# A hybrid decoder layer whose input x also comes transposed from the host, with the first weight tiles used for both token halves at once

## The chip, the cores and the metric

The kernel runs on one core of one Trainium2 chip. The time is device time of one execution in microseconds (us), from a few timed runs; beside it stands one execution recorded by the hardware profiler.

PE is the matrix engine (TensorE), DVE the vector engine, ACT the scalar engine, POOL the GpSimd engine, and SP the queue that issues most loads. Each engine works its instructions off in a fixed order and waits, where it must, at the head of that order. TensorE has two clock levels, 1.2 and 2.4 GHz.

## The reference

The input x has 256 tokens of 2048 features in float32. Three residual stages follow one another, and this study touches only the start of the first:

```python
def swiglu(x, w_gate, w_up, w_down):
    return (jax.nn.silu(x @ w_gate) * (x @ w_up)) @ w_down

def reference(x, ...):
    alpha = (2.0 * DEPTH) ** 0.25
    x = layer_norm(alpha * x + 0.5 * swiglu(x, ffn1_w_gate, ffn1_w_up, ffn1_w_down), ln1_g, ln1_b)
    p = x @ w_in
    mix = concat(diff_attn_group(p[..., :3072], ...), rwkv7_group(p[..., 3072:], ...)) @ w_out
    x = layer_norm(alpha * x + mix, ln2_g, ln2_b)
    return layer_norm(alpha * x + 0.5 * swiglu(x, ffn2_w_gate, ffn2_w_up, ffn2_w_down), ln3_g, ln3_b)
```

The gate and up weights are 2048 x 5632, the down weights 5632 x 2048.

## The kernel before

Nearly all time goes into matrix products of the 256 tokens with streamed weights. The tokens are worked in two halves of 128 (tt = 0 and 1), the weights in column blocks of 512. A block runs over 16 row chunks of 128 (k), two of them per step, so a step loads one weight tile `raw` of 128 x 2 x 512 (512 KB) through SP. To get nearly full float32 precision, each operand is split into a high part of the reduced type fp32r and the rest: ACT copies `raw` to `wh` (line 121), DVE subtracts to get `wl` (line 122), and each product takes three matmuls (lines 103 to 105): high x high, high x rest of the weight, rest of x x high. So one step of one token half is 2 x 3 = 6 matmuls of 512 columns, accumulated in one PSUM bank `acc`; there are 3 such banks.

`raw` has 3 buffers, `wh` and `wl` have 7 each: a load can be issued once the `wl` of three tiles earlier is made, and a `wh` can be written once PE is through with the tile seven earlier. The second token half runs behind the first by LAG = 4 steps (`pend`).

For the matmul x must lie with its features on the partitions. `load_x` loads a piece of 128 tokens x 512 features (256 KB, 8 pieces in all) by hooks at certain steps, `transpose_split` lets PE transpose it in four 128 x 128 pieces into PSUM (line 70), and `split` makes `xh` (line 76, on ACT, and on DVE for the first two pieces) and `xl` (line 77, DVE) from PSUM.

When a gate block ends, ACT makes `sg`, its silu (line 206), out of `acc`; when an up block ends, DVE makes `h` from `sg` and `acc` (line 211), PE transposes it (line 214), and it is split again. The steps run gate block, up block, gate block and so on.

The order of the instructions on each engine isn't the order of the code: a scheduler sets it when the kernel is built, from its own estimate of durations. At the start POOL also loads small constants, and `lp`, `ls`, `le` and `neglam` (lines 293 to 315) are made from them.

Of the kernel before, what the change touches and what calls it, by code (L numbers as in the profile page):

```python
# [10 lines left out]
F32 = mybir.dt.float32  # L11
F32R = mybir.dt.float32r
AF = mybir.ActivationFunctionType
ALU = mybir.AluOpType
AX = mybir.AxisListType

P = 128
D = 2048
S = 256
# [11 lines left out]
LAG = 4  # L31
NW = 7
# [5 lines left out]
def build(tc, A, out):  # L38
# [11 lines left out]
    def nm(s):  # L50
        uid[0] += 1
        return f"{s}_{uid[0]}"
# [14 lines left out]
    def transpose_split(src, tt, q, store, on_dve=False):  # L67
        tr = tr_bank[-1]()
        for j in range(4):
            T.transpose(tr[:, j, :], src[:, j * P:(j + 1) * P], ident)  # L70
        split(tr, store, tt, q, on_dve)
# [12 lines left out]
    class Stream:  # L84
# [24 lines left out]
        def block(self, src, c0, w, ks, lhs, done, budget=0.0):  # L109
            blk = dict(ks=ks, w=w, lhs=lhs, done=done)  # L110
            for ki in range(0, len(ks), 2):
                for f in self.hooks.get(self.step, ()):
                    f()
                self.step += 1
                n = 2
                r0 = ks[ki][0]
                raw = wp.tile([P, n, NB], F32, tag="raw", name=nm("raw"), bufs=NRAW)
                nc.sync.dma_start(out=raw[:, :, :w], in_=src[r0 * P:(r0 + n) * P, c0:c0 + w].rearrange("(k p) n -> p k n", p=P))
                wh = wp.tile([P, n, NB], F32R, tag="wh", name=nm("wh"), bufs=NW)
                wl = wp.tile([P, n, NB], F32R, tag="wl", name=nm("wl"), bufs=NW)  # L120
                SC.copy(out=wh[:, :, :w], in_=raw[:, :, :w])  # L121
                V.tensor_tensor(out=wl[:, :, :w], in0=raw[:, :, :w], in1=wh[:, :, :w].bitcast(F32), op=ALU.subtract)  # L122
                st = (blk, ki, n, wh, wl)
                self.mm(st, 0)
                self.pend.append(st)
                if len(self.pend) > LAG:
                    self.mm(self.pend.pop(0), 1)
                self.run_bg(budget)

# [170 lines left out]
    def mix(mp, pq, C):  # L300
# [16 lines left out]
        # --- evacuation of a column block into channel-major layout  # L317
# [21 lines left out]
        # --- LoRA inputs  # L339
# [108 lines left out]
        def rwkv_group(g, st):  # L448
# [21 lines left out]
            # decay products: exp of sums of log decays, inside a chunk  # L470
# [12 lines left out]
            # keys  # L483
# [30 lines left out]
            # receptance  # L514
# [15 lines left out]
            # pairwise products inside a chunk  # L530
# [9 lines left out]
            # inverses of the 32x32 diagonal blocks, one block per partition  # L540
# [67 lines left out]
            # chunk recurrence  # L608
# [49 lines left out]
            # group norm, bonus, gate  # L658
# [46 lines left out]
        # --- attention  # L705
# [21 lines left out]
        def attn_heads(g, st, heads):  # L727
# [3 lines left out]
            for h in heads:  # L731
# [38 lines left out]
                # mean square in two ranges, so that it overflows to a zero scale as float32 does, with no infinity formed  # L770
# [91 lines left out]
    with tc.tile_pool(name="fp1", bufs=1) as fp, tc.tile_pool(name="pt1", bufs=4, space=bass.MemoryType.PSUM) as pt:  # L862
        tr_bank.append(ffn_bank(pt))
        xc = [fp.tile([P, D], F32, tag=f"y{tt}", name=nm("xc")) for tt in range(2)]

        def load_x(tt, q):
            c = slice(q * NB, (q + 1) * NB)
            nc.sync.dma_start(out=xc[tt][:, c], in_=A["x"][0, tt * P:(tt + 1) * P, c])
            transpose_split(xc[tt][:, c], tt, q, xT, tt == 0 and q < 2)

        for q in range(4):
            stream.hooks[2 * q] = [lambda q=q: load_x(0, q)]
        for q in range(4):
            stream.hooks.setdefault(2 * q + LAG, []).append(lambda q=q: load_x(1, q))
# [15 lines left out]
_INS = ["x", "ffn1_w_gate", "ffn1_w_up", "ffn1_w_down", "ln1_g", "ln1_b", "w_in", "lambda_q1", "lambda_k1",  # L890
# [34 lines left out]
```

## Time and profile before

| | |
|---|---|
| median of 3 runs | 2044.84 us (2044.75 to 2050.93) |
| the profiled execution, first to last instruction (span) | 2040.2 us |
| PE busy | 2005.6 us |
| DVE busy | 1149.2 us |
| ACT busy | 884.8 us |
| moved by DMA | 373.35 MB, mean 183 GB/s |

The profiled execution is known by its span alone; what lies around it (launch and end) is not timed apart. The median of the runs stands 4.6 us above the span. Busy time is the time in which an engine ran at least one instruction. Matmuls overlap in the array: a matmul of 512 columns is shown 0.39 us long, and the next one starts 0.226 us after it, so the distance of two starts is what counts.

### The profile page before, as it was taken

The page shows a single profiled execution, that of the slowest core. Times are in us where ns is not written, and L with a number is a line of the kernel's source. Part 1 is how long each engine was busy: PE and PEld are TensorE (multiplying, and loading weights), DVE is VectorE, ACT ScalarE, POOL GpSimd, SP SyncE. Part 2 cuts the span into 40 slices and gives each one's busy share as a digit, 9 for nine tenths or more (in the row PEclk, how much of TensorE's full clock was granted, in tenths as well). Part 3 has the DMA queues.
Part 4 walks back from the last instruction along what each step waited for, and adds up shares of the span by engine and source line. Part 5 has one row for each costly group of instructions (what it writes and reads, how often), then busy time and mean ns, then how long its engine had stood idle before and what let it go on. Part 6 is the DMA issues. An engine that isn't in the chain of part 4 may idle for free.

```text
span 2040.2 us, 24921 instructions
## 1 busy us (share of the span) xinstructions
PE 2005.6 (98%) x9671; PEld 1631.2 (80%) x9671; DVE 1149.2 (56%) x1419; ACT 884.8 (43%) x1097; POOL 33.5 (2%) x67
## 2 busy tenths in 40 slices
PE   8999999999999999999999989999999999999997
PEld 6888888888888878887778767788888888888886
DVE  5555444445545576776577856755545444454555
ACT  4444443344444337546474533444444334444432
POOL 2000000000000000000000000000000000000000
PEclk9999999999999999999999969999999999999999
DMA  7666656667666556565436715666666666766653
GB/s 248 199 188 192 186 190 201 204 191 228 193 186 190 188 176 194 172 171 154 116 95 175 217 37 174 194 204 187 186 187 192 202 203 196 227 187 186 192 189 124
DMA packets 201992, 373.35 MB, mean 183 GB/s; under 512 B 22810, under 2 KB 24928, under 8 KB 201104
## 3 DMA queue, kind: packets, MB, share of 16 engines
q1 hardware_dynamic: 182912, 350.53, 56.7%
q10 hardware_dynamic: 17440, 14.29, 2.5%
q0 software_dynamic: 1520, 6.93, 0.9%
q8 instruction: 76, 1.25, 0.3%
q14 instruction: 44, 0.36, 0.0%
HBM read 364.10 MB, written 7.60 MB: 182 GB/s over the span
## 4 chain that ended last, share of the span: by engine, by line
PE 90%; DVE 5%; DMA 2%; ACT 1%; issue 1%; SPq 0%; DVEq 0%; ACTq 0%
PE acc L105 28%; PE acc L103 28%; PE acc L104 28%; DVE wl L122 1%; PE tr L214 1%; DMA raw<-in_w_out_dram 1%; PE sm L653 1%; PE sm L650 1%; PE sm L536 1%; DVE y L177 0%; PE tr L325 0%; PE at L741 0%; DMA xc<-in_x_dram 0%; DVE y L178 0%; DVE Y L560 0%
## 5 line engine op out<-in xcount | busy, mean ns | idle before, releaser
L122 DVE TENSOR_TENSOR wl<-raw,wh 128x1024 fp32r<-128x1024 f32 (+1 forms) x664 | 808.1, 1218 | 675.7 <-ACT wh L121 674.7
L121 ACT CAST wh<-raw 128x1024 fp32r<-128x1024 f32 (+1 forms) x664 | 695.1, 1047 | 863.4 <-PE acc L105 752.1
L105 PE MATMUL acc<-wh,xl 128*128 128x512 f32 (+1 forms) x1952 | 742.5, 392 | 1.5 <-DVE xl L77 1.5
L104 PE MATMUL acc<-wl,xh 128*128 128x512 f32 (+1 forms) x1952 | 736.1, 392 | 0.0
L103 PE MATMUL acc<-wh,xh 128*128 128x512 f32 (+1 forms) x1952 | 725.3, 392 | 1.6 <-ACT xh L76 1.2
L103 PEld LDWEIGHTS acc<-wh,xh 128*128 128x128 f32 x1952 | 368.8, 189 | 80.4 <-ACT xh L76 2.7
L105 PEld LDWEIGHTS acc<-wh,xl 128*128 128x128 f32 x1952 | 368.6, 189 | 78.8 <-issue 2.6
L104 PEld LDWEIGHTS acc<-wl,xh 128*128 128x128 f32 x1952 | 368.5, 189 | 75.2 <-issue 0.3
L105 PE MATMUL acc<-wh,hl 128*128 128x512 f32 x704 | 259.3, 397 | 0.0
L104 PE MATMUL acc<-wl,hh 128*128 128x512 f32 x704 | 257.9, 395 | 0.0
L103 PE MATMUL acc<-wh,hh 128*128 128x512 f32 x704 | 255.9, 394 | 0.0
L105 PEld LDWEIGHTS acc<-wh,hl 128*128 128x128 f32 x704 | 132.2, 188 | 32.7
L104 PEld LDWEIGHTS acc<-wl,hh 128*128 128x128 f32 x704 | 132.2, 188 | 32.0
L103 PEld LDWEIGHTS acc<-wh,hh 128*128 128x128 f32 x704 | 132.1, 188 | 31.0
L218 DVE TENSOR_TENSOR hl<-tr,hh 128x512 fp32r<-128x512 f32 x44 | 30.4, 691 | 67.9 <-ACT hh L217 67.9
L217 ACT CAST hh<-tr 128x512 fp32r<-128x512 f32 x44 | 25.8, 587 | 95.7 <-PE tr L214 95.7
L211 DVE SCALAR_TENSOR_TENSOR h<-sg,acc 128x512 f32<-128x512 f32 x44 | 30.3, 688 | 37.2 <-PE acc L105 37.2
L206 ACT ACTIVATE sg<-acc 128x512 f32<-128x512 f32 x44 | 26.4, 599 | 46.1 <-PE acc L105 46.1
L214 PEld LDWEIGHTS tr<-ident,h 128*128 128x128 f32 x176 | 21.8, 140 | 5.7
L214 PE MATMUL tr<-ident,h 128*128 128x128 f32 x176 | 26.4, 272 | 0.0
L558 DVE TENSOR_TENSOR itmp<-U,Y 64x31 f32<-64x31 f32 (+15 forms) x62 | 20.6, 332 | 8.7 <-DMA U<-dU 7.4
L560 DVE TENSOR_TENSOR Y<-Y,itmp 64x31 f32<-64x31 f32 (+15 forms) x62 | 20.6, 331 | 1.3
(240 smaller groups left out, 786.2 us busy)
## 6 DMA issues: line engine op xcount, KB each, us to landing
raw<-in_ffn_w_gate_dram SPq DMA_DIRECT2D x176, 512.0 KB, 3.8
raw<-in_ffn_w_up_dram SPq DMA_DIRECT2D x176, 512.0 KB, 3.8
raw<-in_ffn_w_down_dram SPq DMA_DIRECT2D x176, 512.0 KB, 3.9
raw<-in_w_in_dram SPq DMA_DIRECT2D x96, 512.0 KB, 3.7
raw<-in_w_out_dram SPq DMA_DIRECT2D x32, 512.0 KB, 4.4
rc<-xs ACTq DMA_DIRECT2D x16, 256.0 KB, 4.1
lng<-in_ln_g_dram POOLq DMA_DIRECT2D x3, 1024.0 KB, 6.2
lnb<-in_ln_b_dram POOLq DMA_DIRECT2D x3, 1024.0 KB, 8.8
```

Of the source, the lines that this page charges most:

```text
L103: T.matmul(a, hi, wh[:, j, :w], start=(ki + j == 0), stop=False)
L104: T.matmul(a, hi, wl[:, j, :w], start=False, stop=False)
L105: T.matmul(a, lo, wh[:, j, :w], start=False, stop=(ki + j == last))
L121: SC.copy(out=wh[:, :, :w], in_=raw[:, :, :w])
L122: V.tensor_tensor(out=wl[:, :, :w], in0=raw[:, :, :w], in1=wh[:, :, :w].bitcast(F32), op=ALU.subtract)
L206: SC.activation(out=s, in_=acc, func=AF.Silu)
L211: V.scalar_tensor_tensor(out=h, in0=sg[tt], scalar=0.5, in1=acc, op0=ALU.mult, op1=ALU.mult)
L214: T.transpose(tr[:, i, :], h[:, i * P:(i + 1) * P], ident)
L217: SC.copy(out=hi, in_=tr)
L218: V.tensor_tensor(out=lo, in0=tr, in1=hi.bitcast(F32), op=ALU.subtract)
L558: V.tensor_tensor(out=tv, in0=U[:, 0:j, j:j + 1].to_broadcast([64, j, 32 - j]), in1=Y[:, j:j + 1, j:32].to_broadcast([64, j, 32 - j]), op= ...
L560: V.tensor_tensor(out=Y[:, 0:j, j:32], in0=Y[:, 0:j, j:32], in1=tv, op=ALU.add)
```

## The change

x is put on the host into a second input `xt` of 128 x 16 x 256: the feature inside its chunk on the partition, then the chunk, then the token. Eight pieces of two chunks and all 256 tokens (256 KB each) are loaded straight into that layout, one at each even chunk of the first block, and split from SBUF: `xh` for tt = 0 on DVE, for tt = 1 on ACT, both `xl` on DVE, each instruction 256 columns wide. The 32 transposes of x are gone. The first two steps take one chunk each (256 KB of weights), so the first block has 9 steps, and during the first 20 steps (RAMP) the lag is 0: the code emits the six matmuls of tt = 1 right behind those of tt = 0. The original x is still loaded later for the residual.

```diff
+RAMP = 20
...
-            for ki in range(0, len(ks), 2):
-                for f in self.hooks.get(self.step, ()):
+            ki = 0
+            while ki < len(ks):
+                for f in self.hooks.pop(ki // 2, ()):
                     f()
+                n = 1 if self.step < 2 else 2
+                lag = 0 if self.step < RAMP else LAG
                 self.step += 1
-                n = 2
                 r0 = ks[ki][0]
-                raw = wp.tile([P, n, NB], F32, tag="raw", name=nm("raw"), bufs=NRAW)
+                raw = wp.tile([P, 2, NB], F32, tag="raw", name=nm("raw"), bufs=NRAW)[:, :n]
...
-                if len(self.pend) > LAG:
+                if len(self.pend) > lag:
                     self.mm(self.pend.pop(0), 1)
                 self.run_bg(budget)
+                ki += n
...
-        def load_x(tt, q):
-            c = slice(q * NB, (q + 1) * NB)
-            nc.sync.dma_start(out=xc[tt][:, c], in_=A["x"][0, tt * P:(tt + 1) * P, c])
-            transpose_split(xc[tt][:, c], tt, q, xT, tt == 0 and q < 2)
-
-        for q in range(4):
-            stream.hooks[2 * q] = [lambda q=q: load_x(0, q)]
-        for q in range(4):
-            stream.hooks.setdefault(2 * q + LAG, []).append(lambda q=q: load_x(1, q))
+        xc = [fp.tile([P, 4, 2, S], F32, tag=f"y{i}", name=nm("xc")) for i in range(2)]
+
+        def load_xt(i):
+            xi = xc[i // 4][:, i % 4]
+            nc.sync.dma_start(out=xi, in_=A["xt"][:, 2 * i:2 * i + 2, :])
+            j = slice(2 * (i % 2), 2 * (i % 2) + 2)
+            for tt in range(2):
+                if i % 2 == 0:
+                    xT[(tt, i // 2)] = (xp.tile([P, 4, P], F32R, tag=f"xh{tt}{i // 2}", name=nm("xh")),
+                                        xp.tile([P, 4, P], F32R, tag=f"xl{tt}{i // 2}", name=nm("xl")))
+                hi, lo = xT[(tt, i // 2)]
+                src = xi[:, :, tt * P:(tt + 1) * P]
+                (V.tensor_copy if tt == 0 else SC.copy)(out=hi[:, j], in_=src)
+                V.tensor_tensor(out=lo[:, j], in0=src, in1=hi[:, j].bitcast(F32), op=ALU.subtract)
+
+        for i in range(8):
+            stream.hooks[i] = [lambda i=i: load_xt(i)]
...
+    inputs = dict(inputs, xt=np.asarray(inputs["x"])[0].reshape(S, D // P, P).transpose(2, 1, 0))
```

The scheduler answers with another order on every engine. In the orders below a number behind a name tells buffers apart. Of the changed kernel the weight tiles are, in steps from 0: `wh_104`, 118, 135, 162, 185, 212, 235, 262, 285 (gate), then 307, 327, 345, 363, 381, 399 and so on (up).

The first place is DVE in the first block. Before, the splits of x and of weights follow each other like this:

```order
L122 TENSOR_TENSOR wl_106<-raw_103,wh_105 128x1024
L76 CAST xh_99<-tr_94 128x512
L122 TENSOR_TENSOR wl_119<-raw_116,wh_118 128x1024
L77 TENSOR_TENSOR xl_100<-tr_94,xh_99 128x512
L76 CAST xh_134<-tr_129 128x512
L122 TENSOR_TENSOR wl_141<-raw_138,wh_140 128x1024
L77 TENSOR_TENSOR xl_135<-tr_129,xh_134 128x512
L77 TENSOR_TENSOR xl_169<-tr_163,xh_168 128x512
L77 TENSOR_TENSOR xl_179<-tr_173,xh_178 128x512
L77 TENSOR_TENSOR xl_226<-tr_220,xh_225 128x512
```

In the changed kernel, from just behind the split of tile 2 (`wl_136`) to that of tile 3 (`wl_163`):

```order
L880 CAST xh_152<-xc_87 128x256
L881 TENSOR_TENSOR xl_157<-xc_87,xh_156 128x256
L880 CAST xh_202<-xc_88 128x256
L881 TENSOR_TENSOR xl_207<-xc_88,xh_206 128x256
L881 TENSOR_TENSOR xl_153<-xc_87,xh_152 128x256
L880 CAST xh_202<-xc_88 128x256
L881 TENSOR_TENSOR xl_203<-xc_88,xh_202 128x256
L881 TENSOR_TENSOR xl_207<-xc_88,xh_206 128x256
L881 TENSOR_TENSOR xl_203<-xc_88,xh_202 128x256
L880 CAST xh_252<-xc_88 128x256
L881 TENSOR_TENSOR xl_253<-xc_88,xh_252 128x256
L125 TENSOR_TENSOR wl_163<-raw_160,wh_162 128x1024
```

The splits of later pieces of x (`xh_202`, `xh_252` belong to chunks 8 to 15) now stand ahead of the split of weight tile 3, which multiplies chunks 4 and 5.

The second place is ACT where the first gate block has ended and the up block runs. Before (`wh_289` is the first up tile, `sg_269` the silu of half 0, `sg_370` of half 1):

```order
L121 CAST wh_289<-raw_287 128x1024
L121 CAST wh_308<-raw_306 128x1024
L121 CAST wh_336<-raw_334 128x1024
L121 CAST wh_354<-raw_352 128x1024
L206 ACT_TABLE_LOAD
L206 ACTIVATE sg_269<-acc_109 128x512
L121 CAST wh_374<-raw_372 128x1024
L121 CAST wh_393<-raw_391 128x1024
L206 ACTIVATE sg_370<-acc_194 128x512
```

And in the changed kernel (`wh_307` is the first up tile, `sg_295` and `sg_303` are the silus):

```order
L124 CAST wh_307<-raw_305 128x1024
L317 ACTIVATE le<-ls 128x2
L124 CAST wh_327<-raw_325 128x1024
L124 CAST wh_345<-raw_343 128x1024
L124 CAST wh_363<-raw_361 128x1024
L124 CAST wh_381<-raw_379 128x1024
L210 ACT_TABLE_LOAD
L210 ACTIVATE sg_295<-acc_108 128x512
L124 CAST wh_399<-raw_397 128x1024
L210 ACTIVATE sg_303<-acc_112 128x512
```

Before, the first silu stood behind four up tiles, now it stands behind five.

The third place is PE there. Before, the last matmuls in front of the up block's half 1 (`acc_384`):

```order
L103 MATMUL acc_194<-wh_259,xh_330 128x512
L104 MATMUL acc_194<-wl_260,xh_330 128x512
L105 MATMUL acc_194<-wh_259,xl_331 128x512
L103 MATMUL acc_194<-wh_259,xh_330 128x512
L104 MATMUL acc_194<-wl_260,xh_330 128x512
L105 MATMUL acc_194<-wh_259,xl_331 128x512
L103 MATMUL acc_293<-wh_374,xh_168 128x512
L103 MATMUL acc_384<-wh_289,xh_178 128x512
L104 MATMUL acc_384<-wl_290,xh_178 128x512
```

And in the changed kernel, where half 1 of the up block is `acc_318`:

```order
L104 MATMUL acc_311<-wh_327,xh_94 128x512
L105 MATMUL acc_311<-wl_328,xh_94 128x512
L106 MATMUL acc_311<-wh_327,xl_95 128x512
L104 MATMUL acc_311<-wh_345,xh_152 128x512
L105 MATMUL acc_311<-wl_346,xh_152 128x512
L106 MATMUL acc_311<-wh_345,xl_153 128x512
L104 MATMUL acc_311<-wh_345,xh_152 128x512
L105 MATMUL acc_311<-wl_346,xh_152 128x512
L104 MATMUL acc_318<-wh_307,xh_98 128x512
L105 MATMUL acc_318<-wl_308,xh_98 128x512
```

The first matmul into `acc_318` stands behind 113 other matmuls. Its bank is the one that `acc_108` had, so it waits for `sg_295`. Before, the first matmul into `acc_384` stood behind 121 matmuls (and the transposes of x), and waited in the same way for `sg_269`. Apart from the first 320 rows, PE's order differs only in some 200 rows at the start of the mixers, which hold the same instructions.

## Rows read from the trace of the kernel before

**Rows 1.** The page: busy time and instructions of each engine (part 1), and the shares of the span on the chain of work that ended last (part 4).

```profile
PE 2005.6 (98%) x9671; PEld 1631.2 (80%) x9671; DVE 1149.2 (56%) x1419; ACT 884.8 (43%) x1097; POOL 33.5 (2%) x67
...
PE 90%; DVE 5%; DMA 2%; ACT 1%; issue 1%; SPq 0%; DVEq 0%; ACTq 0%
```

**Rows 2.** The table by stretches of the first 30 us: the stretch, its length, then the busy time of each engine with its instructions in brackets, the granted clock, the busy share of the DMA engines and what they moved in GB/s.

```profile
5.00:10.00 5.00, 1.76 (x9) 1.36 (x8) 2.90 (x3) 2.09 (x2) 2.35 (x5) 1.00 1.04 373
10.00:15.00 5.00, 4.25 (x13) 2.86 (x12) 3.17 (x5) 1.04 (x1) 3.88 (x9) 1.00 1.06 387
15.00:20.00 5.00, 5.00 (x33) 4.27 (x32) 3.17 (x4) 3.87 (x6) 0.42 (x1) 1.00 0.86 264
```

**Rows 3.** The timeline of PE at the start, and around the first transposes of h: start, busy time, line, operation, out<-in and how many; in brackets the idle time before it and what ended it.

```profile
4.57 1.08 PE L70 MATMUL tr<-ident,xc 128*128 128x128 f32 x4 [4.57 <-DMA xc<-in_x_dram]
8.89 1.12 PE L70 MATMUL tr<-ident,xc 128*128 128x128 f32 x4 [3.24 <-DMA xc<-in_x_dram]
9.66 0.78 PE L103 MATMUL acc<-wh,xh 128*128 128x512 f32 x1
...
14.02 0.63 PE L104 MATMUL acc<-wl,xh 128*128 128x512 f32 x1
14.45 0.45 PE L105 MATMUL acc<-wh,xl 128*128 128x512 f32 x1
14.73 0.39 PE L103 MATMUL acc<-wh,xh 128*128 128x512 f32 x1
...
57.07 0.39 PE L104 MATMUL acc<-wl,xh 128*128 128x512 f32 x1
...
58.20 0.39 PE L103 MATMUL acc<-wh,xh 128*128 128x512 f32 x1
58.43 0.60 PE L214 MATMUL tr<-ident,h 128*128 128x128 f32 x4
```

**Rows 4.** The chain of waits, in order of time: start, length, what stood on it.

```profile
18.20 0.44 PE tr L70 x4
```

**Rows 5.** The timeline of ACT, columns as in rows 3.

```profile
5.82 1.04 ACT L121 CAST wh<-raw 128x1024 fp32r<-128x1024 f32 x1 [3.80 <-DMA raw<-in_ffn_w_gate_dram]
7.84 1.04 ACT L121 CAST wh<-raw 128x1024 fp32r<-128x1024 f32 x1 [0.98 <-DMA raw<-in_ffn_w_gate_dram]
10.92 1.04 ACT L121 CAST wh<-raw 128x1024 fp32r<-128x1024 f32 x1 [2.03 <-DMA raw<-in_ffn_w_gate_dram]
...
26.61 1.05 ACT L121 CAST wh<-raw 128x1024 fp32r<-128x1024 f32 x1 [1.74 <-DMA raw<-in_ffn_w_gate_dram]
...
33.58 1.05 ACT L121 CAST wh<-raw 128x1024 fp32r<-128x1024 f32 x1 [1.63 <-DMA raw<-in_ffn_w_up_dram]
...
37.07 1.28 ACT L206 ACT_TABLE_LOAD   x1
38.37 0.60 ACT L206 ACTIVATE sg<-acc 128x512 f32<-128x512 f32 x1
```

**Rows 6.** The timeline of DVE, columns as in rows 3.

```profile
6.89 1.23 DVE L122 TENSOR_TENSOR wl<-raw,wh 128x1024 fp32r<-128x1024 f32 x1 [5.86 <-ACT wh L121]
8.04 0.68 DVE L76 CAST xh<-tr 128x512 fp32r<-128x512 f32 x1
...
26.05 0.28 DVE L293 TENSOR_TENSOR lp<-lq 128x128 f32<-128x128 f32 x1
```

**Rows 7.** The timeline of SP (it issues the loads), its issues at the start and the one at 28.95 us, and the landing time of that one load by the table of DMA issues (size, us from issue to landing); last, the median of all loads of this tensor from the page (part 6).

```profile
0.74 0.39 SPq L868 DMA_DIRECT2D xc<-in_x_dram  x1
1.19 0.94 SPq L118 DMA_DIRECT2D raw<-in_ffn_w_gate_dram  x2
...
3.44 4.73 SPq L868 DMA_DIRECT2D xc<-in_x_dram  x6
8.93 13.29 SPq L118 DMA_DIRECT2D raw<-in_ffn_w_gate_dram  x5
...
28.95 0.37 SPq L118 DMA_DIRECT2D raw<-in_ffn_w_up_dram  x1
...
raw<-in_ffn_w_up_dram SPq DMA_DIRECT2D x1, 512.0 KB, 4.5
...
raw<-in_ffn_w_up_dram SPq DMA_DIRECT2D x176, 512.0 KB, 3.8
```

**Rows 8.** The timeline of PE after an idle stretch at 760 us and after a stretch of small matmuls at 972 us, columns as in rows 3.

```profile
762.63 1.29 PE L70 MATMUL tr<-ident,y 128*128 128x128 f32 x8 [1.95 <-DVE y L178]
...
764.17 0.30 PE L104 MATMUL acc<-wl,xh 128*128 128x288 f32 x1
...
976.93 1.51 PE L741 MATMUL at<-k,q 64*128 64x128 f32 x4
...
978.97 0.63 PE L103 MATMUL acc<-wh,xh 128*128 128x512 f32 x1
...
982.38 0.63 PE L105 MATMUL acc<-wh,xl 128*128 128x512 f32 x1
...
983.77 0.56 PE L104 MATMUL acc<-wl,xh 128*128 128x512 f32 x1
```

**Rows 9.** The table by stretches, columns as in rows 2, of the stretches around rows 8.

```profile
760.00:780.00 20.00, 18.00 (x113) 15.88 (x112) 14.95 (x23) 9.81 (x13) 0.24 (x1) 1.00 0.70 221
...
950.00:1000.00 50.00, 50.00 (x348) 37.64 (x347) 30.81 (x75) 21.75 (x58) 2.03 (x2) 0.93 0.44 126
```

More of the change, by code (lines that the diff above doesn't have):

```diff
@@ L110, in block @@
             blk = dict(ks=ks, w=w, lhs=lhs, done=done)
-            for ki in range(0, len(ks), 2):
-                for f in self.hooks.get(self.step, ()):
-                    f()
+            ki = 0
+            while ki < len(ks):
+                for f in self.hooks.pop(ki // 2, ()):
+                    f()
+                n = 1 if self.step < 2 else 2
+                lag = 0 if self.step < RAMP else LAG
                 self.step += 1
-                n = 2
                 r0 = ks[ki][0]
-                raw = wp.tile([P, n, NB], F32, tag="raw", name=nm("raw"), bufs=NRAW)
+                raw = wp.tile([P, 2, NB], F32, tag="raw", name=nm("raw"), bufs=NRAW)[:, :n]
                 nc.sync.dma_start(out=raw[:, :, :w], in_=src[r0 * P:(r0 + n) * P, c0:c0 + w].rearrange("(k p) n -> p k n", p=P))
-                wh = wp.tile([P, n, NB], F32R, tag="wh", name=nm("wh"), bufs=NW)
-                wl = wp.tile([P, n, NB], F32R, tag="wl", name=nm("wl"), bufs=NW)
+                wh = wp.tile([P, 2, NB], F32R, tag="wh", name=nm("wh"), bufs=NW)[:, :n]
+                wl = wp.tile([P, 2, NB], F32R, tag="wl", name=nm("wl"), bufs=NW)[:, :n]
                 SC.copy(out=wh[:, :, :w], in_=raw[:, :, :w])
@@ L863, in build @@
         tr_bank.append(ffn_bank(pt))
-        xc = [fp.tile([P, D], F32, tag=f"y{tt}", name=nm("xc")) for tt in range(2)]
-        def load_x(tt, q):
-            c = slice(q * NB, (q + 1) * NB)
-            nc.sync.dma_start(out=xc[tt][:, c], in_=A["x"][0, tt * P:(tt + 1) * P, c])
-            transpose_split(xc[tt][:, c], tt, q, xT, tt == 0 and q < 2)
-        for q in range(4):
-            stream.hooks[2 * q] = [lambda q=q: load_x(0, q)]
-        for q in range(4):
-            stream.hooks.setdefault(2 * q + LAG, []).append(lambda q=q: load_x(1, q))
+        xc = [fp.tile([P, 4, 2, S], F32, tag=f"y{i}", name=nm("xc")) for i in range(2)]
[13 more added lines that the diff above has]
+            stream.hooks[i] = [lambda i=i: load_xt(i)]
         xr = [A["x"][0, t * P:(t + 1) * P, :] for t in range(2)]
@@ L887, in build @@
     ctx.close()
-_INS = ["x", "ffn1_w_gate", "ffn1_w_up", "ffn1_w_down", "ln1_g", "ln1_b", "w_in", "lambda_q1", "lambda_k1",
+_INS = ["x", "xt", "ffn1_w_gate", "ffn1_w_up", "ffn1_w_down", "ln1_g", "ln1_b", "w_in", "lambda_q1", "lambda_k1",
         "lambda_q2", "lambda_k2", "attn_norm_g", "rwkv_mu", "rwkv_w0", "rwkv_w2", "rwkv_a0", "rwkv_a2", "rwkv_g2",
```

## The prediction

> **What bounds the kernel now.** I read the page first: PE is busy 2005.6 of 2040.2 us and holds 90% of the chain that ended last [rows 1]. So the time is the number of matmuls times the distance of two starts, plus whatever PE loses. The change leaves the number of matmuls alone (the 32 transposes of x apart) and reorders only the first 60 us and a stretch at the start of the mixers. So only what PE loses there matters. The table by stretches shows it: from 5 to 10 us PE is busy 1.76 us, while the DMA engines are full (share 1.04, 373 GB/s), and from 15 us on PE has no gap [rows 2].
>
> I put one number on this loss. Around 57 us two starts lie 0.226 us apart (five distances from 57.07 to 58.20), and the first transposes of h start at 58.43 [rows 3]. By the order of before, 190 matmuls stand ahead of them: 190 x 0.226 = 42.9. PE has lost 58.4 - 42.9 = 15.5 us by then: waiting for x (4.57 us, then 3.24), matmuls at the low clock level (0.43 apart from 14.02 to 14.45, against 0.23 after 14.73) [rows 3], and the transposes, 0.44 for four [rows 4], 3.5 for all 32.
>
> **What goes, and what the start costs instead.** Tiles are numbered as in the change. The transposes and their waits go, and so do splits out of PSUM. The first matmul can start when the first piece of xt, tile 0, and their splits are there, near 6 us instead of 9.66. But then DMA decides. SP's loads land about in the order of their issue: 0.26 MB by 4.57, 0.79 by 5.82, 1.31 by 7.84, 2.10 by 10.92 [rows 3, 5], from there 387 GB/s [rows 2]. The changed order has eight pieces of xt, 0.26 MB each, between the tiles: tile 2 is complete at 1.57 MB (8.9 us), and six pieces and tiles 0 to 3 make 3.15 MB: 10.92 + 1.05 / 0.387 = 13.6 us. The half tiles take two issues more at some 0.45 us each (0.94 for two, [rows 7]), hidden behind the full DMA engines.
>
> Next is DVE. A weight split takes 1.23 us for 1024 columns, the 128 columns of lp 0.28 [rows 6], so 0.15 + columns / 960: 0.42 us for 256 columns, about 0.37 when the next one follows closely (8.04 begins 0.08 before 6.89 + 1.23 ends). The weight split of tile 2 waits for ACT (8.9 + 1.05) and stands behind a piece of xt that lands at 9.9, so it ends at about 12.2. Then twelve splits of x come ahead of tile 3's: 12 x 0.37 = 4.4 (eleven of them stand in the order shown, one just ahead of it), so `wl_163` runs from 16.6 to 17.85, though its load is there at 13.6 and its cast done at 14.7. PE has then done 26 matmuls; it waits until 17.85 and has lost 17.85 - 26 x 0.226 = 12.0. The low clock level at the start disappears in that wait, since PE is ahead of the tiles anyway.
>
> The nearest row for a copy on DVE is from PSUM, 0.68 for 512 columns [rows 6], the same one element per cycle. The Trainium skill, "VectorE: DVE Perf Modes" (The perf-mode tier table), says that a float32 tensor_copy between SBUF buffers runs at twice that rate and a tensor_tensor doesn't; no row here shows such a copy. By that rule the four copies among the twelve would save some 0.14 us each, and the sum below would be about 0.6 us better.
>
> **What is late next.** Three raw buffers make a loop: a load is issued when the split three tiles earlier ends, lands after 4.5 us (issue at 28.95) or 3.8 (median of all) [rows 7], and needs 1.05 on ACT and 1.23 on DVE. That is 6.1 to 6.8 us for three tiles; before, 26.61 to 33.58 on ACT is 7.0 for three [rows 5]. Before, PE met this loop at full lag, with the silu far ahead of its need: `sg` starts at 38.37 [rows 5], and PE asks for that bank only after 121 matmuls and all transposes, at about 43.
>
> Now the first silu stands on ACT behind tile 13, and tile 13 hangs on the loop twice over: the split of tile 4 ends at 17.85 + 3 x 0.37 + 1.23 = 20.2; tile 7 one turn later, tile 10 another; then the load of tile 13, its cast 1.05, the table load 1.28 and the silu 0.60 [rows 5]. With 4.5 per load this ends at 20.2 + 2 x 6.8 + 4.5 + 2.9 = 41.2, with 3.8 at 39.1. Loads came closer than 3 us to each other there before and took the longer time, but a loop with gaps of its own takes the shorter; I take the middle, 40.2. PE is through the 113 matmuls ahead of `acc_318` at 12.0 + 113 x 0.226 = 37.5 and stands for 2.7 us. What it has lost by then is 40.2 - 25.5 = 14.7. Queued behind that matmul is all of PE's work, and behind the silu on ACT the cast of tile 14, which PE needs only 43 matmuls later: 9.7 us of cover. A loss of up to 2.7 us before that point costs nothing, because the loop sets the end of the wait.
>
> After it nothing is late: half 1 leaves more tiles ready than PE uses, and where the lag goes from 0 to 4 PE uses four tiles at half their matmuls, 1.36 us each, with seven buffers filled. The transposes of h of both halves come together there, behind 21 matmuls of the next block, which cover the 0.7 of DVE. The mixers' rearranged start holds the same instructions; PE is idle 2.0 us there between 760 and 780 [rows 9], so it bounds gain and loss at 2.0 each, and I take 0.
>
> **Sum.** 15.5 lost before, 14.7 after: 0.8 us gained. Against its own execution: 2040.2 - 0.8 = 2039.4 us of span. The median of the runs is 4.6 above the span, so 2044.0 us. The bounds: 41.2 for the silu gives -0.2, 39.1 gives +1.9; with the mixers from -2.2 to +3.9, so 2041 to 2047.
>
> **Rivals.** First, clearly faster: the silu isn't late. If the x splits run at half price or the scheduler's place for them does no harm, tile 3 is split at 13.6 + 1.05 + 1.23 = 15.9, PE has lost 10.0 and the loop runs 2 us earlier, with 3.8 per load to 37.1; PE, at 10.0 + 25.5 = 35.5, then waits 1.6. Lost 11.6, gained 3.9: 2040.9. For it: DVE has room between 10 and 15 us (3.17 of 5, [rows 2]). Against it: the splits stand in the order, and DVE does not overtake.
>
> Second, slower: the wait at `acc_318` lowers TensorE's clock. Rows show both answers. After an idle stretch of 1.95 us at 760 matmuls still ran at the high level [rows 8]; after a stretch of small matmuls before 976.93, matmuls of 512 columns ran 0.43 apart from 978.97 to 982.38, and the mean clock of that stretch is 0.93 [rows 8, 9]. The price is that of the same episode: 976.9 to 983.8 at half speed loses 3.4 us. With the silu at its late end (1.0 more) the time is 2044.0 + 4.4 = 2048.4. It decides once the wait is longer than the 1.95 us that left the clock alone; 2.7 is expected. The Trainium skill, "TensorE: Matmul & The Clock Gate" (HAM oscillation), has the same mechanism, a wait between matmuls that puts the clock back; rows 8 agree for one of two cases.
>
> That the change doesn't do what it says is partly so and already in the sum: the order gives the first 17 matmuls of the up block to half 0 alone.
>
> **How the numbers follow.** Forecast (a gain of 0.8, 2042 to 2046): 0.66. Faster rival: 0.18. Slower rival: 0.16. A difference of 0.3%, 6.1 us, is about what a measurement of this kernel can tell from none (its runs lie between 2044.75 and 2050.93). None of the three cases reaches that alone. Faster than 2038.7 needs the first rival and the mixers' 2 us: 0.08. Slower than 2051.0 needs the second and the mixers' 2 us: 0.07. Within: 0.85. The range takes both rivals in: 2040.5 to 2048.5.
>
> **What would show it.** In the changed trace: the first matmul near 6 us; PE idle for 2 to 3 us before the split of tile 3 (`wl_163`) ends at about 17.9, with DVE full of 256-column splits from 10 to 17; PE idle again for 2 to 3 us near 38, released by `sg` on ACT, which ends near 40; the first transposes of h behind 213 matmuls at about 14.7 + 213 x 0.226 = 62.8. Wrong would be: no wait for `sg`, tile 3 split before 16, matmuls 0.43 apart after 40, or a difference that comes from the mixers.

## The result and the profile after

The changed kernel takes 2049.34 us (median of 20 runs, 2043.3 to 2054.9), the kernel before in the same job 2043.97 (20 runs, 2038.17 to 2050.93): ratio 1.0024, interval 1.0015 to 1.0033. That is 5.4 us slower, where a gain of 0.8 was forecast: inside the 0.3% that was called no change, but above the range given, and on the other side of 1. The profiled execution has a span of 2047.6 us. The page of the changed kernel, parts 1 and 4 (against [rows 1]):

```profile
PE 2008.1 (98%) x9639; PEld 1632.0 (80%) x9639; DVE 1151.5 (56%) x1434; ACT 886.1 (43%) x1100; POOL 33.5 (2%) x67
...
PE 89%; DVE 5%; DMA 3%; ACT 2%; issue 1%; SPq 0%; DVEq 0%; ACTq 0%
```

PE does 32 instructions less and is busy 2.5 us longer. So either matmuls ran slower or they were started later; the table by stretches says both (columns as in [rows 2]: PE first, the granted clock third from the end):

```profile
5.00:10.00 5.00, 4.62 (x11) 3.62 (x12) 2.44 (x5) 1.35 (x3) 2.44 (x5) 1.00 0.95 324
...
15.00:20.00 5.00, 3.32 (x14) 2.27 (x14) 4.93 (x12) 3.03 (x5) 0.36 (x1) 1.00 0.83 211
35.00:40.00 5.00, 2.90 (x13) 2.06 (x11) 3.35 (x3) 3.17 (x3) 0.00 (x0) 1.00 0.71 218
40.00:45.00 5.00, 4.13 (x11) 3.23 (x12) 2.62 (x3) 3.32 (x6) 0.00 (x0) 0.68 0.75 217
45.00:50.00 5.00, 5.00 (x23) 4.13 (x22) 2.42 (x2) 2.47 (x3) 0.00 (x0) 0.98 0.80 243
```

From 5 to 10 us PE now works 4.62 us where it worked 1.76 [rows 2]. In exchange it idles from 15 to 20 and from 35 to 40, and from 40 to 45 it does 11 matmuls at a granted clock of 0.68; a full stretch holds 23. The timeline of PE (columns as in [rows 3]) has the places one by one:

```profile
5.38 1.22 PE L104 MATMUL acc<-wh,xh 128*128 128x512 f32 x2 [5.38 <-ACT wh L124]
...
13.09 0.50 PE L105 MATMUL acc<-wl,xh 128*128 128x512 f32 x1 [0.99 <-DVE wl L125]
...
17.88 0.50 PE L105 MATMUL acc<-wl,xh 128*128 128x512 f32 x1 [1.68 <-DVE wl L125]
...
40.87 0.50 PE L104 MATMUL acc<-wh,xh 128*128 128x512 f32 x1 [2.97 <-ACT sg L210]
...
41.67 0.55 PE L104 MATMUL acc<-wh,xh 128*128 128x512 f32 x1
42.02 0.63 PE L105 MATMUL acc<-wl,xh 128*128 128x512 f32 x1
...
45.00 0.71 PE L106 MATMUL acc<-wh,xl 128*128 128x512 f32 x2
45.55 0.40 PE L104 MATMUL acc<-wh,xh 128*128 128x512 f32 x1
...
65.31 1.04 PE L218 MATMUL tr<-ident,h 128*128 128x128 f32 x8
```

PE stands 2.97 us at `acc_318` until the first silu is there; some 0.8 us later the starts are 0.43 apart (42.02 to 45.00), that is the lower of the two levels, until 45. The first transposes of h come at 65.31, before at 58.43 [rows 3], with 23 matmuls more ahead of them (213 against 190). The silu on ACT, against [rows 5]:

```profile
37.87 1.04 ACT L124 CAST wh<-raw 128x1024 fp32r<-128x1024 f32 x1 [1.15 <-DMA raw<-in_ffn_w_up_dram]
38.93 1.28 ACT L210 ACT_TABLE_LOAD   x1
40.22 0.60 ACT L210 ACTIVATE sg<-acc 128x512 f32<-128x512 f32 x1
```

It stands behind the fifth up tile as the order said, and that tile's load is what came last. DVE around the split of tile 3, against [rows 6]:

```profile
11.82 1.22 DVE L125 TENSOR_TENSOR wl<-raw,wh 128x1024 fp32r<-128x1024 f32 x1
12.96 0.42 DVE L881 TENSOR_TENSOR xl<-xc,xh 128x256 fp32r<-128x256 f32 x1
...
14.74 0.28 DVE L880 CAST xh<-xc 128x256 fp32r<-128x256 f32 x1
...
16.61 1.22 DVE L125 TENSOR_TENSOR wl<-raw,wh 128x1024 fp32r<-128x1024 f32 x1
```

**How to split a difference of 0.2%.** Single runs of either kernel spread over 10 us and more, so two helps were used below. The first is a mark: the moment when SP issues its first load of `w_in`, the end of the first stage as SP sees it. Three profiles of the kernel before have it at 734.39, 734.16 and 733.47 us (mean 734.0), four of the changed kernel at 735.96, 734.88, 735.26 and 736.65 (mean 735.7). SP's timeline of the first profile of each, the kernel before first, has the mark and the first load of `w_out`, the next mark (start, time until SP was through, how many):

```profile
734.39 372.26 SPq L118 DMA_DIRECT2D raw<-in_w_in_dram  x104
1110.35 151.74 SPq L118 DMA_DIRECT2D raw<-in_w_out_dram  x32
```

```profile
735.96 376.25 SPq L121 DMA_DIRECT2D raw<-in_w_in_dram  x104
1115.91 153.18 SPq L121 DMA_DIRECT2D raw<-in_w_out_dram  x32
```

The second help is the mean granted clock that each run lists beside its span. The low level is half the clock, so span - span x clock is half of the time at the low level: what that level costs if PE has work all that time. It is an account and not a measured loss: in the first profile of before PE is through at 2028.4, the clock is still low behind that (0.80 from 2020 to 2040), and nothing there waits for PE.

### The profile page after: what moved, and what is told of

Its sections match the earlier page's. It is cut to its first block, busy times and chain, and to the rows that moved or that the text cites. A ratio compares the mean times of both kernels' runs of the same rounds, so it can differ in the third digit from the quotient of the medians.

```text
span 2047.6 us, 24876 instructions
## 1 busy us (share of the span) xinstructions
PE 2008.1 (98%) x9639; PEld 1632.0 (80%) x9639; DVE 1151.5 (56%) x1434; ACT 886.1 (43%) x1100; POOL 33.5 (2%) x67
## 4 chain that ended last, share of the span: by engine, by line
PE 89%; DVE 5%; DMA 3%; ACT 2%; issue 1%; SPq 0%; DVEq 0%; ACTq 0%
PE acc L106 28%; PE acc L104 28%; PE acc L105 28%; DVE wl L125 1%; PE tr L218 1%; ACT wh L124 1%; DMA raw<-in_w_out_dram 1%; PE sm L657 1%; PE sm L654 1%; PE sm L540 1%; DMA raw<-in_w_in_dram 0%; DVE y L181 0%; PE at L745 0%; DVE y L182 0%; DMA xc<-in_xt_dram 0%
```

## The experiments

Marks and waits are those of each run's one profile; ratios are against the kernel before on the same chip, behind the first job 11 or 12 runs against 29 to 35.

| run | ratio, interval | first load of w_in | PE's wait for sg |
|---|---|---|---|
| changed kernel, first job | 1.0024, 1.0015 to 1.0033 | 735.96 | 2.97 |
| e1_again, e6_again, e10_again: the same | 0.9998, 0.9982 to 1.0013; 1.0027, 1.0014 to 1.0040; 1.0018, 1.0005 to 1.0032 | 734.88; 735.26; 736.65 | 2.6; 3.2; 3.4 |
| e5_before, e16_before: before | 1.0005, 0.9994 to 1.0016; one run | 734.16; 733.47 | none |
| e2_ramp17: lag 0 for 17 steps | 1.0005, 0.9992 to 1.0018 | 736.06 | 2.95 |
| e3_ramp9, e11_ramp9: for 9 steps | 0.9993, 0.9978 to 1.0007; 0.9989, 0.9976 to 1.0002 | 731.64; 731.18 | none |
| e12_ramp0: lag 4 throughout | 0.9991, 0.9979 to 1.0003 | 732.96 | none |
| e4_bank: another bank | 0.9996, 0.9980 to 1.0012 | 733.14 | none |
| e7_raw20: half tiles in other buffers | 0.9996, 0.9981 to 1.0011 | 734.62 | 1.4 |
| e8_fill: 24 matmuls more | one run | 736.06 | under 0.1 |
| e13_n2: no half tiles | 0.9984, 0.9972 to 0.9996 | 731.68 | 0.5 |
| e14_lag: lag 0 alone | 0.9995, 0.9983 to 1.0007 | 732.94 | none |
| e9_raw9, e15_raw9: e7 with 9 steps | 0.9983, 0.9973 to 0.9992; 0.9981, 0.9967 to 0.9994 | 730.21; 729.70 | none |

**First job: is it the mixers' other order, or the start?** In these four, theory A blames the mixers' order and theory B the start and the clock. From e5 on, A is the start, and further letters are told in each text. The unchanged kernel again:

> The changed kernel once more, unchanged, as the yardstick of the other three. Both theories: the first load of w_in (end of the first FFN's loads) near 736.0 us of the profile against 734.4 before, PE waiting some 3 us for sg near 38 and matmuls 0.43 apart behind it; a ratio to before of 1.0015 to 1.0033. From w_in to the end the profile of before took 1305.8 us and that of after 1311.6: theory A (the mixers' other order costs time) expects 1309 or more again; theory B (this part differs from run to run and the order costs nothing) expects anything from 1304 to 1312.

Then two lengths of the stretch with lag 0; 17 keeps PE's wait for the late silu, 9 puts more matmuls ahead of it. (What the texts of e2_ramp17 and e4_bank say of the mixers' order doesn't hold; the traces are read behind e4_bank.)

```diff
-RAMP = 20
+RAMP = 17
```

> Lag 0 for the first 17 steps instead of 20. The start up to there keeps its order (half 1 of the up block behind 113 matmuls and the silu behind five up tiles), but the mixers' order comes out as in the kernel before. Both theories: the same wait of some 3 us for sg and the same w_in mark of about 736. Theory A (1.6 us lost at the start, some 3 lost by the mixers' order): ratio to before about 1.0008, and 1306 us from w_in to the end. Theory B (the mixers' order costs nothing, the start and what follows from its clock costs all): ratio about 1.0024 as in the changed kernel.

```diff
-RAMP = 20
+RAMP = 9
```

> Lag 0 for the first 9 steps only (the first gate block), so the up block's half 1 waits for four tiles and stands behind 126 matmuls; the mixers' order is that of the changed kernel. At the start PE should wait for single tiles instead of once for sg, by less than 2 us at a time, with no fall of the clock: w_in mark 734 to 735. Theory A (the mixers' order costs some 3 us): ratio 1.0010 to 1.0020, 1309 us or more from w_in to the end. Theory B: ratio 0.9995 to 1.0003.

And half 1 of the first up block in a PSUM bank of the transposes, so that it need not wait for the silu:

```diff
-                self.acc[tt] = pa.tile([P, NB], F32, tag="acc", name=nm("acc"))
+                self.acc[tt] = (tr_bank[-1]().rearrange("p a b -> p (a b)") if blk["no"] == 1 and tt == 1 else
+                                pa.tile([P, NB], F32, tag="acc", name=nm("acc")))
```

> The changed kernel, but half 1 of the first up block accumulates in one of the four PSUM banks of the transposes, so that it need not wait for the silu; the mixers' order comes out as in the kernel before. Both theories: no wait for sg near 38 and no fall of the clock, PE has lost 12.0 us at the start instead of 15.5 before, so the w_in mark falls to about 731 and the ratio to about 0.9983. If the wait is not what costs the time at the start, the mark stays near 736.

The traces contradict one premise of these texts: e2_ramp17 and e4_bank don't have the mixers' order of before. By the names of tiles, PE, DVE and ACT go through the mixers in the changed kernel's order in e2_ramp17, e3_ramp9, e4_bank, e11_ramp9 and e12_ramp0, and in that of before in e8_fill and e13_n2; e7_raw20, e9_raw9 and e15_raw9 share a third order, e14_lag has a fourth. One place is enough to see it: between the two lines below PE does 5 matmuls of 512 columns in the kernel before, and 9 in e2_ramp17 as in the changed kernel.

```profile
790.02 1.02 PE L463 MATMUL sm<-tw,Q 64*128 64x256 f32 x4
...
792.42 0.66 PE L325 MATMUL tr<-ident,tm 128*128 128x128 f32 x4
```

```profile
792.91 1.02 PE L467 MATMUL sm<-tw,Q 64*128 64x256 f32 x4
...
796.12 0.66 PE L329 MATMUL tr<-ident,tm 128*128 128x128 f32 x4
```

So this job doesn't set one order against the other. Theory A's number still failed: it had 1309 us or more from `w_in` to the end with the changed order, and e1_again takes 1307.3, e3_ramp9 1308.1. From the first load of `w_in` to that of `w_out`, e3_ramp9 takes 375.9 us with the changed order, no more than the 376.0 of the first profile of before; e2_ramp17 and e4_bank take 380.1 with the same order. So the order alone needn't cost anything there; whether it can is taken up below. In the first stage the picture is regular: with the wait for sg the mark is 734.9 or later, without it 731.6 and 733.1. In e4_bank the wait only moved: PE then stood 2.0 us at the first transposes of h. The ratio of e2_ramp17, close to theory A's 1.0008, decides nothing, since the changed kernel itself has 0.9998 in that job.

The surprise was e1_again, 0.9998 for the kernel that had 1.0024. So the next jobs carry the kernel before as a kernel of its own, and the changed kernel again.

> The kernel before, run against itself. It tells what a ratio means whose two sides are the same program, and how far its stretches vary from one execution to the next. Theory C (the first comparison's 1.0024 is mostly a difference in how often the granted clock fell, which varies between jobs and executions whatever the kernel): the ratio lies within 0.999 to 1.001, its spans spread over some 10 us with the mean granted clock, and the stretch from the first load of w_in to that of w_out, 376.0 us in the first profile, may as well come out near 380. Theory D (the change itself makes the mixers and what follows 4 to 6 us slower): this stretch is 376 us again and the whole from w_in to the end 1305 to 1307 us.

> The changed kernel once more, in a job that also has the kernel before as a kernel of its own, so that the mean granted clocks of both can be set side by side. Theory C: the ratio is between 0.999 and 1.002, and span times mean clock (the span that full clock would give) differs from that of before by under 1.5 us. Theory D: the ratio is 1.002 to 1.003 as in the first comparison. Both: PE waits 2.5 to 3.0 us for sg at acc_318, matmuls are 0.43 apart for some 3 us behind it, and the first load of w_in is issued between 734.5 and 736.2 us.

> The changed kernel a fourth time, beside its variants on one chip. Theory C (all of the difference is chance): ratio 0.999 to 1.001. Theory G (a fixed part of 1.0 to 1.6 us by the first load of w_in, from the wait at acc_318 and the low level behind it, another 1.6 us from a fall of the clock at 762 to 768 us that the kernel before doesn't have, and chance of some 2 us on top): ratio 1.0005 to 1.003, first load of w_in between 734.8 and 736.1 us.

The same program against itself gives 1.0005, and its stretch from w_in to w_out came out at 378.4 where the first profile had 376.0, as theory C had it and D had not (from w_in to the end it takes 1306.4, inside D's 1305 to 1307). But the changed kernel gives 1.0027 and 1.0018, so the difference isn't all chance either; theory G came nearest, though the mark of e10_again, 736.65, lies above its 736.1. Over the 56 runs of the changed kernel and 139 of before whose clock is listed (all but those of before in the first job and e16_before), the means are:

| | span | span x clock | span - span x clock |
|---|---|---|---|
| before | 2041.5 | 2013.4 (standard error 0.2) | 28.1 (0.4) |
| changed | 2045.4 | 2013.6 (0.3) | 31.8 (0.7) |

By this account the work and its waits cost the same in both, and 3.7 of the 3.9 us belong to the low level. Run by run it costs less than the account says: 1 us more in the last column goes with 0.60 us more span over the runs of before and with 0.76 over those of the changed kernel (fitted lines). At that rate, an estimate, the low level has 2.2 to 2.8 of the 3.9 us.

**Does the wait bring the low level?** 24 matmuls into the up block's own bank, wiped out by its first real one, keep PE busy until the silu is there:

```diff
+            if blk["no"] == 1 and tt == 0 and ki == 0:
+                for i in range(FILL):
+                    T.matmul(acc, blk["lhs"](0, 0)[0], wh[:, 0, :], start=True, stop=True)
```

> The changed kernel with 24 more matmuls of 512 columns ahead of the first up block, into its own bank and wiped out by the block's own first matmul, so that PE is busy until the first silu ends and doesn't stand idle at the first matmul of half 1. Only the granted clock behind that place is the question. Theory A (the idle wait lowers the clock): matmuls from 41 to 46 us stay 0.226 apart, the stretch from 40 to 45 us has a granted clock of 1.00 (0.68 in the changed kernel). Theory E (the clock falls there for another reason, such as the start's sum of waits): the stretch shows 0.7 again. The first load of w_in: 24 x 0.226 = 5.4 us more work, less the wait of 2.7 and, by theory A alone, less 1.6 us of low clock: 736.9 by A, 738.5 by E.

Table by stretches and timeline of PE of e8_fill:

```profile
40.00:45.00 5.00, 4.94 (x22) 4.05 (x22) 2.45 (x2) 3.36 (x5) 0.00 (x0) 1.00 0.79 246
45.00:50.00 5.00, 5.00 (x24) 4.14 (x23) 2.91 (x3) 2.31 (x3) 0.00 (x0) 1.00 0.77 236
```

```profile
33.07 5.60 PE L105 MATMUL acc<-wh,xh 128*128 128x512 f32 x24
...
39.65 0.39 PE L111 MATMUL acc<-wh,xl 128*128 128x512 f32 x1
40.09 0.50 PE L109 MATMUL acc<-wh,xh 128*128 128x512 f32 x1
40.43 0.39 PE L110 MATMUL acc<-wl,xh 128*128 128x512 f32 x1
```

The clock stays at 1.00 (0.68 in the changed kernel), and starts are 0.23 apart in place of 0.43: theory A holds, E falls. The mark, 736.06, is 0.8 under what A worked out. The wait is what lowers the clock at this place, by five profiles with it and one with it filled.

**What makes the silu late?** Three edits take one part of the change each. First the half tiles' raw weights in two free buffers, so that they don't occupy two of the three raw buffers:

```diff
-                raw = wp.tile([P, 2, NB], F32, tag="raw", name=nm("raw"), bufs=NRAW)[:, :n]
+                raw = (wp.tile([P, 2, NB], F32, tag="raw", name=nm("raw"), bufs=NRAW)[:, :n] if n == 2 else
+                       self.small().rearrange("p (a b) -> p a b", a=1))
...
+        stream.small = lambda: fp.tile([P, NB], F32, tag="sg", name=nm("raw"), bufs=2)
```

> The changed kernel with one thing more: the raw weights of the two half tiles go into two free buffers of 128 x 512 (the later home of sg), so that the three raw buffers belong to whole tiles from the start. The load of tile 3 is then issued ahead of the fourth piece of xt, the split of tile 3 stands behind two splits of x on DVE and no longer behind twelve, and the first silu stands on ACT behind three up tiles and no longer behind five. Theory A (the start loses its gain at tile 3 and at the silu, and the wait for the silu lowers the clock): tile 3 is split before 15.5 us, no wait of over 1 us for sg, no matmuls 0.43 apart between 38 and 46, the first load of w_in between 729 and 732 us (735.5 in the changed kernel), and the median 3 to 6 us under that of the changed kernel. Theory B (the silu waits for the stream of weights as a whole, whatever the start's order): sg ends at 40 again and the first load of w_in stays over 734.

The load of tile 3 is issued at 3.60 in place of 6.07, and the silu ends at 36.4 (40.8 in the changed kernel). But the timeline of PE of e7_raw20 shows where the gain went:

```profile
36.48 0.50 PE L104 MATMUL acc<-wh,xh 128*128 128x512 f32 x1 [1.41 <-ACT sg L211]
...
62.24 1.16 PE L219 MATMUL tr<-ident,h 128*128 128x128 f32 x8 [1.85 <-DVE h L216]
63.16 0.63 PE L104 MATMUL acc<-wh,xh 128*128 128x512 f32 x1
63.59 0.63 PE L105 MATMUL acc<-wl,xh 128*128 128x512 f32 x1
...
66.58 0.47 PE L106 MATMUL acc<-wh,xl 128*128 128x512 f32 x1
```

The sg wait of 1.41 leaves the clock alone. But with lag 0 through the up block both halves' h are asked for at once, PE stands 1.85 us, and the low level comes there. The mark, 734.62, missed theory A's 729 to 732 by that. Then the half tiles left out, and, on the kernel before, the lag alone (with the x of half 1 loaded at once):

```diff
-                n = 1 if self.step < 2 else 2
+                n = 2
```

> The changed kernel without its two half tiles: 8 whole steps in the first block, lag 0 for 20 steps. By its order the first silu stands on ACT behind four up tiles (five in the changed kernel), and the mixers' order on PE is that of the kernel before. Theory A (the place of the silu on ACT sets the wait): PE waits for sg between 0.5 and 2.5 us (3.0 to 3.4 in the changed kernel), the first load of w_in comes between 733.5 and 735.5 us. Theory I (the clock's fall near 762 comes with the changed kernel's own order of the mixers): none here. Theory J (it comes with either order, by the moment): it may show, as it did in e12_ramp0 with this same order.

```diff
-                if len(self.pend) > LAG:
+                if len(self.pend) > (0 if self.step <= RAMP else LAG):
...
-            stream.hooks.setdefault(2 * q + LAG, []).append(lambda q=q: load_x(1, q))
+            stream.hooks.setdefault(2 * q, []).append(lambda q=q: load_x(1, q))
```

> The kernel before with the lag of 0 for the first 20 steps alone, and the x of half 1 loaded at once for it: transposes and whole tiles stay. Theory A (the lag of 0 brings the first silu into PE's way): a wait for sg of 2 us or more near 40, matmuls 0.43 apart behind it, the first load of w_in at 736 to 740 us, and the median 2 to 6 us over that of before. Theory K (the late silu is the work of the changed order of splits and raw buffers): no wait for sg over 1 us, the first load of w_in at 733 to 735.

```diff
-RAMP = 20
+RAMP = 0
```

> The changed kernel with the lag of 4 from the first step, as before: only x by xt and the two half tiles are left of the change. Theory A (the lag of 0 is what makes the first silu late; the transposed x alone gains): no wait for sg, no fall of the clock before 70 us, first load of w_in 1 to 4 us earlier than in the kernel before (730.5 to 733.4). Theory H (the lag of 0 is what makes use of the first tiles, without it PE starves on them): first load of w_in at 734 us or later.

ACT, DVE and PE of e13_n2:

```profile
34.85 1.05 ACT L124 CAST wh<-raw 128x1024 fp32r<-128x1024 f32 x1 [0.41 <-DMA raw<-in_ffn_w_up_dram]
35.93 1.28 ACT L210 ACT_TABLE_LOAD   x1
37.22 0.60 ACT L210 ACTIVATE sg<-acc 128x512 f32<-128x512 f32 x1
```

```profile
10.55 1.22 DVE L125 TENSOR_TENSOR wl<-raw,wh 128x1024 fp32r<-128x1024 f32 x1
...
12.79 1.23 DVE L125 TENSOR_TENSOR wl<-raw,wh 128x1024 fp32r<-128x1024 f32 x1 [0.36 <-ACT wh L124]
...
18.30 1.23 DVE L125 TENSOR_TENSOR wl<-raw,wh 128x1024 fp32r<-128x1024 f32 x1
```

```profile
37.87 0.50 PE L104 MATMUL acc<-wh,xh 128*128 128x512 f32 x1 [0.47 <-ACT sg L210]
38.21 0.40 PE L105 MATMUL acc<-wl,xh 128*128 128x512 f32 x1
```

Without half tiles the weights of chunks 4 and 5 are split at 12.79 to 14.02 (16.61 to 17.83 in the changed kernel). The later x splits stand behind that tile and take their time from the next one. The silu stands behind four up tiles, ends at 37.82, PE waits 0.47 us and the clock holds. The mark is 731.68, better than expected and 4.0 us better than the changed kernel's mean, and the kernel is faster than before, 0.9984. Lag 0 alone brought no wait for sg at all (e14_lag: theory A fell, K held, mark 732.94). Half tiles with lag 4 brought none either (e12_ramp0, 732.96). So in these variants the long wait takes both: half tiles in the raw buffers and the lag of 0 for 17 or 20 steps. Theory A of e12_ramp0 missed one point: behind a wait of 1.24 us the clock falls at the start (0.66 from 12 to 14 us). So it does in e4_bank behind waits of 0.85 and 1.05 (0.68).

**Both mends.** e9_raw9 joins the edits of e7_raw20 and e3_ramp9; e11_ramp9 is e3_ramp9 again beside it.

> The changed kernel with both mends at once: the raw weights of the two half tiles in two free buffers, as in e7_raw20, and the lag of 0 only for the first 9 steps, as in e3_ramp9. Theory A (what the change gains at the start it loses at the silu, and e7_raw20 lost it again at the first transposes of h, where both halves came together): neither wait is there, the clock stays at its high level from 40 to 70 us, the first load of w_in is issued between 728 and 731 us (734.2 to 734.4 in the kernel before), and the median is 2 to 6 us under that of before. Theory F (PE is held at the start by the stream of weights in any case, and the loss only moves): some other wait of 2 us or more shows before 70 us and the first load of w_in stays at 733 or later.

> The kernel of e9_raw9 on another chip. If its gain is real: first load of w_in between 729 and 731 us again, ratio 0.997 to 0.9995. If e9_raw9 was a lucky set of runs: ratio 0.9995 or more.

> The changed kernel with a lag of 0 for 9 steps in place of 20, a second time, beside the changed kernel on one chip. Theory A: no wait for sg, first load of w_in between 731 and 732.5 us, and spans 3 to 6 us shorter than those of the changed kernel in this job. Theory C: the start's 4 us drown in the spread, no difference of medians over 2 us.

PE of e9_raw9, all the waits that the view shows before 56 us, and the first transposes of h:

```profile
5.58 1.22 PE L104 MATMUL acc<-wh,xh 128*128 128x512 f32 x2 [5.58 <-ACT wh L125]
...
12.39 0.50 PE L105 MATMUL acc<-wl,xh 128*128 128x512 f32 x1 [1.19 <-DVE wl L126]
...
21.57 0.51 PE L105 MATMUL acc<-wl,xh 128*128 128x512 f32 x1 [0.53 <-DVE wl L126]
...
54.03 0.60 PE L219 MATMUL tr<-ident,h 128*128 128x128 f32 x4
```

This version beats the kernel before on two chips, 0.9983 and 0.9981 with both intervals below 1, and the changed kernel on the one chip where both ran (medians 2039.64 and 2045.48). Theory F fell. Span x clock is 2011.5 and 2011.4 against 2013.7 and 2013.0 of before in the same jobs, and what the span has beyond that is 26.0 and 27.2 against 26.6 and 29.5. So by that account the gain lies mainly in the work and the waits on the first chip, 2.2 of 2.8 us, and only in part on the second, 1.6 of 3.9. Beside the changed kernel, e11_ramp9 has spans 5.9 us shorter in the mean (2038.0 against 2043.8), as theory A had it.

**Is a second low stretch, near 762 us, the change's?** All four profiles of the changed kernel have it, the first two of before don't. One line each, from 740 to 780 us, of the changed kernel, of before, and of e16_before:

```profile
740.00:780.00 40.00, 37.10 (x208) 32.07 (x207) 29.89 (x48) 15.18 (x23) 2.04 (x2) 0.96 0.62 185
```

```profile
740.00:780.00 40.00, 37.13 (x215) 31.81 (x214) 31.61 (x51) 16.57 (x24) 2.03 (x2) 1.00 0.64 190
```

```profile
740.00:780.00 40.00, 36.41 (x205) 31.51 (x204) 30.45 (x48) 15.63 (x24) 2.03 (x2) 0.96 0.59 177
```

> The kernel before, one more profile, for two things alone. The first load of w_in: 734.0 to 734.6 us, as in its two profiles so far, by the theory that the first stage hardly varies. The clock between 760 and 770 us: 1.00 as in both so far by theory I (the fall there belongs to the changed order); by theory J it may show here too.

The kernel before can have it too (0.04 x 40 = 1.6 us), and so has e13_n2 with its order of the mixers (0.96), while e4_bank has the changed order without it (1.00). Theory I fell; J holds. (The text of e13_n2 takes e12_ramp0 for an example with the order of before; its trace has the changed order.) (The mark of this profile, 733.47, also lies outside the 734.0 to 734.6 expected: the first stage of before varies by 0.9 us.) Whether the change makes it likelier stays open: 4 of 4 profiles against 1 of 3, and by the mixers' order 8 of 9 against 2 of 5.

## Why the prediction was wrong

**The start was right, partly by luck.** First matmul near 6: 5.38. Tile 3 split at 17.85: 17.83. But tile 2's split ended at 13.04, not 12.2, and the twelve splits took 16.61 - 12.96 = 3.65 us, not 4.4; the two errors cancel. The Trainium skill, "VectorE: DVE Perf Modes" (The perf-mode tier table), covers most of the second: by it the prediction estimated 0.6 us less for the four copies, and the trace agrees, with 0.28 for a copy of 256 columns from SBUF and 0.42 for the subtraction.

**The wait was right.** PE was through at 40.87 - 2.97 = 37.9 (37.5 forecast). The silu ended at 40.82, and in the four profiles between 39.76 and 40.82 (40.2 forecast). The forecast, without the clock, was a gain of 0.8; span x clock, by the account above, says a loss of 0.2 with a standard error of 0.4.

**The clock was the step that failed.** The slower rival named this place and gave its condition: a wait longer than 1.95 us, with 2.7 expected. By its own terms it was the likeliest case, but it got 0.16, and the sum has nothing for the low level. Its mechanism came in all five profiles with a wait of 2.6 to 3.4 us (four of the changed kernel and e2_ramp17), and e8_fill took it away. Its price, 3.4, was too high: from 42.02 to 45.00 seven distances were 0.43 in place of 0.226, and with the edges 0.32 x 5 = 1.6 us were lost in the stretch from 40 to 45. The first 13 matmuls behind the wait took 4.68 us there; in e10_again they took 5.64, so it lost about 2.6. The first transposes of h, forecast at 62.8, came at 64.2 to 66.0. By the mark the change costs 1.7 us (735.7 against 734.0) where 0.8 was to be gained, and most of that turn of 2.5 is the clock's 1.6 to 2.6. The Trainium skill, "TensorE: Matmul & The Clock Gate" (HAM oscillation), has this mechanism, a wait between matmuls that puts the clock back, and the runs agree: 0.68 behind the wait, 1.00 with the wait filled. The rows behind the prediction had shown it in neither case: the wait of 1.95 us left the level alone, and the fall at 977 stood behind small matmuls with PE busy throughout (50.00 of 50.00, [rows 9]).

**"Hidden" was wrong for the half tiles.** The prediction priced them as two issues of 0.45 us behind full DMA engines. Their real price is a buffer each: a half tile occupies a whole one of three raw buffers, the load of tile 3 waits for it, DVE takes up x splits ahead of it, and the silu falls one tile further back. e13_n2, which leaves the half tiles out altogether, shows it at 4.0 us at the mark, the low level included. The buffers alone are worth 1.1 with a lag of 0 for 20 steps (e7_raw20) and some 1.5 with 9 (e9_raw9 and e15_raw9 against e3_ramp9 and e11_ramp9). The late split and the late silu were in the sum, by the order; what the prediction missed is that the half tiles bring them about.

**The term for the mixers was off as well, by these few profiles, and why stays open.** The prediction took 0 for their rearranged start, with bounds of 2.0. From the first load of `w_in` to that of `w_out` the four profiles of the changed kernel take 379.7 to 380.0 us, the three of before 376.0, 378.4 and 378.1: 2.3 us more in the mean. Behind that the two differ by 0.4. With the 1.7 at the mark this makes the 4.4 us by which these profiles differ, and over all runs it was 3.9. By the granted clock from 740 to 780 and from 930 to 1110, some 1.8 of the 2.3 are again the low level's (6.5 us in the account in place of 4.7). Whether the mixers' order brings it is not shown. Against it stand e3_ramp9 and e11_ramp9, which have that order and take 375.9 and 375.8. For it, six of the nine profiles with that order take 379.7 or more, and none of the five with the order of before more than 378.4. No run changes the order alone.

Part of the first job's 5.4 us is chance: the same kernel had 0.9998 in another job. The range, which ended at 2048.5, allowed for none of that spread: one run of the kernel before had already stood at 2050.93 among the three known then.

## What to carry to other kernels

Where a stream runs through few buffers, a smaller first piece still costs a whole buffer: give it one of its own, or the load behind it comes late. Where PE is the bound, price a wait that a change creates with the low level behind it, and make that the forecast where the wait is longer than those that the trace shows as harmless. For differences of 0.2%, put spans beside their mean clock and compare marks inside the profile before any cause is named, and take more than one profile of the kernel before.

## What the runs showed of the hardware

The length of a wait alone doesn't say whether the clock falls. Waits of 1.41 (e7_raw20), 1.95 and 2.4 (before and e5_before, at 762) and 2.0 us (e4_bank) left the level alone. Waits of 1.24 (e12_ramp0, at the start), 1.85 (e7_raw20, before the transposes of h), 1.99 and 2.7 (the changed kernel and e16_before, at 762) lowered it, and so did all five of 2.6 to 3.4 for sg. The low stretches that PE saw after them lasted some 3 to 5 us. What else decides is open.

In every kernel span - span x clock is 26 to 33 us of 2040 in the mean of its runs, so some 52 to 67 us pass at the low level. About half of that or more lies between 1140 and 1260 us (granted clock 0.82 to 0.91 there). It varies from run to run with a standard deviation of 4.4 us in the kernel before and 5.0 in the changed one (of the 26 to 33), and most of the spread of these runs goes with it.

The column of the granted clock is no guide at the very start: it has 1.00 from 10 to 15 us in the kernel before [rows 2], where starts are 0.43 apart from 14.02 to 14.45 [rows 3].
